# Follow-up steps as own streams, another start, and full-row sample-state products in a hybrid decoder layer

## The chip, the cores and the metric

The kernel runs on one core of a Trainium2 chip. The metric is the device time of one execution, in microseconds. The kernel before took 2090.97 us as the median of three runs (2090.45 to 2092.82).

A core has a matrix engine (TensorE, PE in the profile, with its weight loads as PEld), VectorE (DVE), ScalarE (ACT) and GpSimd (POOL) for elementwise work, and SyncE (SP), which here only issues DMA transfers. Matrix products are collected in PSUM, which has eight banks; everything else lies in SBUF or in device memory.

## The reference

One decoder layer over 1088 tokens: 1024 of a prompt and 64 of a sample group (8 sequences with 8 new tokens, each with 4096 cached tokens in pages).

```
z = x @ w_in                       # 1024 -> 13 parts (q_a k_a v_a q_i k_i w_i q_b k_b v_b g_b a_b gate_a gate_b)
scores = sum_h relu(q_i[h] . k_i) * w_i[h]      # indexer, 8 heads of 64
keys   = the 256 best keys per query            # prompt: causal; sample: the cache and the new tokens
attn   = softmax(q_a . k_a[keys]) @ v_a[keys]   # 8 heads, 2 key heads
log_a  = log_sigmoid(a_b @ w_alpha2 + b) / 16   # per key channel
o_b    = gated linear attention(q_b, k_b, v_b, log_a, state)    # 4 heads, 128 x 256, returns the new state
o_b    = rms_norm(o_b) * g * silu(g_b)
mixed  = (sigmoid(gate_a) * (attn @ w_attn_o) + sigmoid(gate_b) * (o_b @ w_gla_o)) @ w_out
h = layer_norm(alpha * x + mixed);   y = layer_norm(alpha * h + relu(h @ w_ff1)^2 @ w_ff2)
```

It returns y, the new keys, values and indexer keys, and the new states, all in float32.

## The kernel before

**Products.** Each large product is made of three on rounded parts: an operand is split in a high part (h, a rounded copy, ScalarE) and a low part (l, the rest, by a subtraction on VectorE or GpSimd), and h.h, l.h and h.l are added up in one PSUM bank (mm3, L620). Activations lie feature by feature with the tokens along the row, in three chunks of 384, 384 and 320 tokens (CH, L36). One weight tile of 1024 x 128 is thus 8 x 3 products per chunk.

**Jobs.** The projection of x is a list of jobs, one for each weight tile: job 0 (misc: indexer keys, indexer weights and a_b), jobs 1 to 4 (qi, indexer queries), then qa, ka, va, the linear attention's qb, kb, vb, gates of the branch (gb), and the merge gates (gate), with the merge's products (pmb, pma) and the output projection (pwo) behind them. main() (L1701) runs the jobs in order; w_load and w_split read and split weights ahead of their job. fmajor (L629) is one job's chunk.

**Streams.** What depends on results beside the jobs is written as generators: the indexer of the prompt and of the sample (idx_prompt, idx_sample), three searches for the 256th best score (top_first: ga and gb, two groups of prompt queries; top_second; top_sample: gs), the masks made from them, the linear attention (gla, gla_pre), softmax (at_soft) and the value products (at_pv). A search halves an interval: it counts scores over a threshold on VectorE (jk) and ScalarE (jka, jkb) and sets the next threshold in short VectorE steps. The sample search spreads its scores over all partitions and adds the counts up in one small product a step (ppr).

**Order.** No engine chooses its order at run time. A planner (Clock, Stream and Order, L97 to L320) runs the generators against a table of costs and writes one fixed instruction order for each engine. A generator yields the tiles that it needs next. A stream is due when they are ready by the planner's clock, and no earlier than its engines' planned times less a slack:

```
return max([c.ready(x) + self.margin for x in self.need] + [c.t[e] - self.slack for e in self.engines] + [0.0])
```

At each step the first stream of the list that is due goes (L299); a stream with engines=() waits for its tiles alone. PSUM banks go round by last use, and a pinned bank isn't given away. Waits between engines come from tile dependencies. On every queue, SP's too, an instruction that waits holds all behind it.

**Places the change touches.** The start: SP reads the page table, the page rows (ptg), weight 0, x chunk by chunk in pairs of rows, and weight 1 behind chunk 0 (L424 to L480); x is split as it comes; POOL gathers cached indexer pages into cig and SP writes them out (ci_s) to read them again in another layout. The sample state of the linear attention (sample in gla, L1212): pus = k.v for 8 sequences, with 128 rows of k for v's high part and the 64 rows that are not zero for its low part:

```
pe.matmul(pu[:, x * 256:(x + 1) * 256], kz[:, 2 * j + x, :], vh, start=True, stop=False)
pe.matmul(pu[:, x * 256:(x + 1) * 256], kz[:TS, 2 * j + x, :], vl[:TS], start=False, stop=True)
```

The reads of the linear attention's output for the merge (ob_load, L1555: obl, eight blocks, first chunk 0 and then chunks 1 and 2 together, split into obh and obl). The last layer norm of the kernel (ln_last, L1919): sums of y and y squared per token by products with a matrix of ones (plv, pld), the root and its reciprocal, and the product plr which lays the factors along rows.

Nearly every instruction has line L256 in the profile: it is the call in Engine that records it for the planner. So tile names tell places apart.

Of the kernel before, what the change touches and what calls it, by code (L numbers as in the profile page):

```python
# [23 lines left out]
P = 128  # L24
# [3 lines left out]
KT = 8  # L28
# [21 lines left out]
NSH = 6  # L50
# [9 lines left out]
NAHL = 4  # L60
# [20 lines left out]
NGATE = 4  # L81
WLATE = 4.0
# [292 lines left out]
def front(ph, tc, env, A, O):  # L375
# [37 lines left out]

    def scale_rows(x, r):
# [9 lines left out]
    sp.dma_start(ptab, view(A["page_table"], 0, [[0, P], [32, 8], [1, 32]]))  # L424
    ptg = cst("ptg", [P, 2], I32)
    sp.dma_start(ptg, A["page_rows"])
# [3 lines left out]
    def w_load(i):  # L430
        src, kt, m = jobs[i][0]
        pages = []
        for k0 in range(0, kt, 1024 // m):
            kn = min(1024 // m, kt - k0)
            r = page(f"wr{i}_{k0}", F32, [P, kn, m])
            sp.dma_start(r, src[:, k0:k0 + kn, :])
# [3 lines left out]
    def w_split(i):  # L440
        for n, e in enumerate(wt[i]):
# [4 lines left out]
            sub(l, r, f32(h), WLATE if 1 < state["job"] < mix_at - 1 else 0.0)  # L446
            e[0], e[1] = h, l

    state = {"dma": 0, "split": 0, "job": 0}

    def w_get(i):
# [6 lines left out]
        hs, ls = [], []  # L458
        for h, l, kn in wt.pop(i):
            for k in range(kn):  # L460
                hs.append(h[:, k, :])
                ls.append(l[:, k, :])
# [6 lines left out]
    state["dma"] = 1  # L469
# [3 lines left out]
    for c, (c0, n) in enumerate(CH):  # L473
        for k in range(0, KT, 2):
            xr[k, c] = page(f"xr{k}{c}", F32, [P, 2, 384])
            sp.dma_start(xr[k, c][:, :, :n], A["xT"][k:k + 2, :, c0:c0 + n].rearrange("k p t -> p k t"))
        if c == 0:
            w_load(1)
            state["dma"] = 2
# [16 lines left out]
    for g in range(8):  # L496
        dve.tensor_scalar(ix_i[:, g], ptg, 8.0, float(g), op0=OP.mult, op1=OP.add)
    ix_k = const("ix_k", [1, 256], I32)
    dve.tensor_scalar(ix_k, ptab[0:1].rearrange("p a b -> p (a b)"), 128.0, None, op0=OP.mult)
# [32 lines left out]

    for c, (c0, n) in enumerate(CH):
        for k in range(KT):
            s = slice(c0, c0 + n)
# [3 lines left out]
            if c == 0 and k == 0:  # L539
                w_split(0)  # L540
                state["split"] = 1
# [103 lines left out]
    def to_stacks(ps, c, st):  # L645
# [5 lines left out]
        for e in range(2):  # L651
            own, oth = slice(e * 64, e * 64 + 64), slice(64 - e * 64, 128 - e * 64)
            dve.tensor_sub(st[e][oth, c0:c0 + n], ps[own, :n], f32(st[e][own, c0:c0 + n]))
# [4 lines left out]
    def qi_job(f):  # L658
        def run(w):
            st = [page(f"qi{2 * f + e}", F32R) for e in range(2)]  # L660
            for c in range(3):
                ps = yield from fmajor(w, c, f"qi{f}_{c}")
                to_stacks(ps, c, st)
# [4 lines left out]
    def misc_job(w):  # L668
        for c in range(3):
            c0, n = CH[c]  # L670
            ps = yield from fmajor(w, c, f"misc{c}")
# [10 lines left out]
        sp.dma_start(O["kidxT"], misc[0:64])  # L682
        flags.add("misc")
# [11 lines left out]
    def qa_job(f):  # L695
        def run(w):
            st = [page(f"qa{2 * f + e}", F32R) for e in range(2)]
            for c in range(3):
                ps = yield from fmajor(w, c, f"qa{f}_{c}")
                to_stacks(ps, c, st)  # L700
# [55 lines left out]
    def idx_sample():  # L756
# [30 lines left out]
        def chunk(p, kh, kl, n):  # L787
# [7 lines left out]
            dve.scalar_tensor_tensor(rl[:, :n], ps[:, :n], 0.0, f32(rh[:, :n]), op0=OP.max, op1=OP.subtract)  # L795
            return rh, rl

        def sums(p, r, n, po, first, last):
            rh, rl = r
# [4 lines left out]
        for qq in range(4):  # L804
            po = [bank("po0", True), bank("po1", True)]
            pend = None
            for p in range(4):
# [7 lines left out]
                for e in range(2):  # L815
# [3 lines left out]
                    if pend:  # L819
                        yield [pend[1][1]]  # L820
                        sums(*pend)
                    pend = (p, r, 512, po[e], p == 0, p == 3)
            yield [pend[1][1]]
# [8 lines left out]
        for p in range(4):  # L832
            r = chunk(p, kkn[:, 0], kkn[:, 1], 64)
            yield [r[1][:, :64]]
# [140 lines left out]
    def masks(g, qts, gte):  # L975
        for i, grp in enumerate(MKP if not mk else ()):
# [207 lines left out]
    def gla(h):  # L1184
# [17 lines left out]
        dve.tensor_sub(vl[:TS], vs[:TS], f32(vh[:TS]))  # L1202
        qz = small("gqz", 512).rearrange("p (a b) -> p a b", b=TS)
# [8 lines left out]
        def sample():  # L1212
# [4 lines left out]
            for i in range(2):  # L1217
# [8 lines left out]
                for j in range(2):  # L1226
                    yield [kz, vh, vl[:TS]]
                    pu = bank("pus")
                    for x in range(2):
                        pe.matmul(pu[:, x * 256:(x + 1) * 256], kz[:, 2 * j + x, :], vh, start=True, stop=False)  # L1230
                        pe.matmul(pu[:, x * 256:(x + 1) * 256], kz[:TS, 2 * j + x, :], vl[:TS], start=False, stop=True)
                    for x in range(2):
                        b = 2 * j + x
                        la = g["lasts"][:, 4 * i + b:4 * i + b + 1]
                        u = small("us", 256)
                        act.activation(u, pu[:, x * 256:(x + 1) * 256], AF.Copy, scale=la)
                        dve.scalar_tensor_tensor(st[i][:, b, :], st[i][:, b, :], la, u, op0=OP.mult, op1=OP.add)
                sp.dma_start(O["gla_s"][4 * i:4 * i + 4, h].rearrange("b k v -> k b v"), st[i])
# [3 lines left out]
            act.activation(vs[:TS], po[:TS, :256], AF.Copy)  # L1242

# [21 lines left out]
        for ci in range(8):  # L1265
# [20 lines left out]
            else:  # L1286
                S2 = small("S", 256)
                dve.scalar_tensor_tensor(S2, S, g["last"][:, ci:ci + 1], u, op0=OP.mult, op1=OP.add)
                S = S2
            if ci < 7:  # L1290
                Sm = small("Sm", 256)
                act.activation(Sm, S, AF.Copy, scale=g["mid"][:, ci + 1:ci + 2])
# [26 lines left out]

    def g_job(h, j):  # L1320
        def run(w):
# [3 lines left out]
            for c in range(3):  # L1325
                c0, n = CH[c]
                pg = yield from fmajor(w, c, f"gb{h}{j}_{c}")
                t = small("gt")
# [8 lines left out]
                dve.scalar_tensor_tensor(t[:, :n], t[:, :n], 1.0, pg[:, :n], op0=OP.add, op1=OP.mult)  # L1337
                dve.scalar_tensor_tensor(t[:, :n], po[:, :n], gn5[:, j:j + 1], t[:, :n], op0=OP.mult, op1=OP.mult)
                sp.dma_start(ob_s[2 * h + j][:, c0:c0 + n], t[:, :n])
        return run  # L1340

# [40 lines left out]
    def at_soft():  # L1382
# [7 lines left out]
        def norm(x):  # L1390
            rc = tiny("rc", 1)
            dve.reciprocal(rc, x[3][:, 3:4])
            scale_rows(x[2][:, :(x[0][0] + 1) * P], rc)
# [6 lines left out]
        for i, (qt, hp) in enumerate(units):  # L1400
# [11 lines left out]
            for h in range(2):  # L1412
# [18 lines left out]
                if len(fly) > 2:  # L1431
                    yield [fly[0][3][:, 3:4]]
                    norm(fly.popleft())
# [1093 lines left out]
```

## Time and profile before

| | |
|---|---|
| median of three runs | 2090.97 us (2090.45 to 2092.82) |
| the profiled execution | 2094.44 us, span 2092.7 us |
| mean granted TensorE clock | 0.987 |
| TensorE busy | 2039.7 us (97%) in 12443 instructions |
| VectorE busy | 1261.8 us (60%) |
| ScalarE busy | 1121.3 us (54%) |
| GpSimd busy | 774.9 us (37%) |
| DMA | 264.51 MB, mean 126 GB/s |

Times are those of one profiled execution. In a row of the timeline stand the start in us, the length in us, engine, line, operation, out<-in by tile names without their numbers, shape, and in brackets the idle time before it with what ended it; rows with "x8" are eight in a row. A matmul's length overlaps that of the next, so the distance of two starts is what a product costs. A product in float32 that is not rounded shows as two records. The granted clock is 1.00 at full rate and 0.50 at half.

### The profile page before, as it was taken

To read this page: it belongs to the slowest core of one execution; us is meant where nothing else is said; L and a number is where in the kernel's file an instruction comes from. 1 tells how busy PE (TensorE), PEld (TensorE's weight loads), DVE (VectorE), ACT (ScalarE), POOL (GpSimd) and SP (SyncE) were. 2 spreads that over 40 slices of the span, in tenths; PEclk is the share of its full clock that TensorE was granted. 3 is DMA by queue.
4 is the path that set the end of the run, shared out by engine and by line. 5 is a ranking of instruction groups with operands and counts; after the bars stand their busy time and mean duration, and the time that the engine had idled before them with its cause. 6 is when DMAs were issued, how large, how long until landed. Compare 5 with 4: busy or idle time off the path is not lost.

```text
span 2092.7 us, 34594 instructions
## 1 busy us (share of the span) xinstructions
PE 2039.7 (97%) x12443; PEld 1965.4 (94%) x12443; DVE 1261.8 (60%) x2630; ACT 1121.3 (54%) x2222; POOL 774.9 (37%) x579
## 2 busy tenths in 40 slices
PE   7999999999799999999999999999999999999998
PEld 7989999898789999999999899999899999999997
DVE  6976776756845666753167844565654453566635
ACT  5678777787567765674023424455353242445543
POOL 3344121212221113113134324565655343354455
PEclk9999999999899999999999999999999999999998
DMA  6664301212023224245473234655533343235542
GB/s 237 260 188 140 124 21 51 95 34 92 23 72 127 83 83 139 84 135 196 170 277 121 71 89 130 188 155 166 148 100 111 122 130 107 66 129 163 186 151 89
DMA packets 185596, 264.51 MB, mean 126 GB/s; under 512 B 22208, under 2 KB 119488, under 8 KB 185424
## 3 DMA queue, kind: packets, MB, share of 16 engines
q1 hardware_dynamic: 177872, 236.87, 35.1%
q0 software_dynamic: 7552, 25.43, 3.9%
q8 instruction: 98, 1.61, 0.3%
q14 instruction: 74, 0.61, 0.1%
HBM read 212.72 MB, written 49.51 MB: 125 GB/s over the span
## 4 chain that ended last, share of the span: by engine, by line
PE 87%; DVE 5%; issue 4%; POOL 2%; ACT 2%; DMA 1%; SPq 0%; ACTq 0%; POOLq 0%; DVEq 0%
PE pf L256 32%; PE gate L256 9%; PE gb L256 5%; PE pwo L256 4%; PE psv L256 4%; PE pmb L256 4%; PE qb L256 2%; PE kb L256 2%; PE qa L256 2%; PE po L256 2%; PE qi L256 2%; PE psc L256 2%; PE pma L256 2%; PE psq L256 2%; PE pov L256 2%
## 5 line engine op out<-in xcount | busy, mean ns | idle before, releaser
L256 PE MATMUL pf<-a,w 128*128 128x384 f32 (+1 forms) x2304 | 397.4, 328 | 2.3 <-POOL a L256 1.3
L256 PE MATMUL pf<-h,w 128*128 128x384 f32 (+1 forms) x2304 | 396.4, 329 | 3.0 <-POOL w L256 1.7
L256 PEld LDWEIGHTS pf<-h,w 128*128 128x128 f32 x2304 | 380.9, 189 | 5.6 <-POOL w L256 2.1
L256 PEld LDWEIGHTS pf<-a,w 128*128 128x128 f32 x2304 | 378.4, 188 | 6.6 <-POOL a L256 1.8
L256 POOL TENSOR_TENSOR wl<-wr,wh 128x1024 fp32r<-128x1024 f32 (+1 forms) x66 | 150.6, 2283 | 470.0 <-ACT wh L256 415.1
L256 POOL TENSOR_TENSOR w<-wr,w 128x512 fp32r<-128x512 f32 x142 | 202.2, 1433 | 130.6 <-ACT w L256 122.0
L256 ACT ACTIVATE w<-wr 128x512 fp32r<-128x512 f32 x272 | 156.5, 618 | 62.2 <-PE pwo L256 25.8
L256 DVE TENSOR_TENSOR w<-wr,w 128x512 fp32r<-128x512 f32 x130 | 135.0, 1046 | 52.7 <-ACT w L256 52.4
L256 DVE TENSOR_TENSOR acc<-acc,pf 128x384 f32<-128x384 f32 (+1 forms) x136 | 72.9, 538 | 94.9 <-PE pf L256 92.9
L256 PE MATMUL gate<-xh,wh 128*128 128x384 f32 (+1 forms) x384 | 129.9, 338 | 0.0
L256 PE MATMUL gate<-xh,wl 128*128 128x384 f32 (+1 forms) x384 | 125.5, 327 | 0.0
L256 PE MATMUL gate<-xl,wh 128*128 128x384 f32 (+1 forms) x384 | 125.4, 327 | 0.0
L256 POOL TENSOR_TENSOR a<-fr,a 128x384 fp32r<-128x384 f32 (+1 forms) x54 | 52.6, 974 | 195.0 <-ACT a L256 188.5
L256 ACT ACTIVATE wh<-wr 128x1024 fp32r<-128x1024 f32 (+1 forms) x75 | 74.4, 1006 | 76.2 <-DMA wr<-wgo 39.4
L256 DVE TENSOR_TENSOR fr<-fr,pf 128x384 f32<-128x384 f32 (+1 forms) x96 | 50.8, 529 | 91.8 <-ACT fr L256 91.5
L256 ACT ACTIVATE fr<-pf 128x384 f32<-128x384 f32 (+1 forms) x96 | 44.9, 467 | 114.2 <-PE pf L256 112.7
L256 ACT ACTIVATE a<-fr 128x384 fp32r<-128x384 f32 (+1 forms) x96 | 48.7, 507 | 81.1 <-DVE fr L256 79.1
L256 DVE TENSOR_SCALAR_CACHE_REDUCE jk<-sc,ga_f 128x1024 int8<-128x1024 f32 (+2 forms) x96 | 88.4, 921 | 2.1
L256 ACT ACTIVATE jkb<-sc,gb_f 128x896 int8<-128x896 f32 (+2 forms) x96 | 86.0, 896 | 4.4 <-DVE gb_f L256 2.7
L256 DVE TENSOR_TENSOR phl<-ppt,phl 128x512 fp32r<-128x512 f32 (+1 forms) x80 | 50.2, 637 | 60.4 <-ACT phl L256 59.9
L256 PE MATMUL psv<-wh,xh 128*128 128x256 f32 (+1 forms) x288 | 83.8, 291 | 0.0
L256 PE MATMUL psv<-wl,xh 128*128 128x256 f32 (+1 forms) x288 | 81.2, 282 | 0.0
(507 smaller groups left out, 5182.9 us busy)
## 6 DMA issues: line engine op xcount, KB each, us to landing
wr<-wff SPq DMA_DIRECT2D x256, 256.0 KB
wr<-w SPq DMA_DIRECT2D x43, 512.0 KB
ckr<-kT SPq DMA_DIRECT2D x256, 64.0 KB
ga_s<-gate SPq DMA_DIRECT2D x16, 544.0 KB
ci_s<-cig SPq DMA_DIRECT2D x16, 512.0 KB
kir<-ci_s SPq DMA_DIRECT2D x16, 512.0 KB
wr<-wout SPq DMA_DIRECT2D x13, 512.0 KB
mgp<-ga_s SPq DMA_DIRECT2D x16, 384.0 KB
```

The costliest lines, as they stand in the source:

```text
L256: r = f(*a, **k)
```

## The change

**Start.** Weight 0 is read in two halves, each ahead of a pair of x rows; the rest of x's chunk 0 follows, then weight 1 and the page rows, x's chunks 1 and 2, and last the page table. TensorE makes 28 transposes of the identity into a bank that nobody reads (warm). Weight 0 is split half by half between the rows of x, weight 1 after chunk 0, both by ScalarE and VectorE. Jobs 0 and 1 alternate by chunk: misc 0, qi 0, misc 1, qi 1, misc 2, qi 2.

**Follow-ups.** The second halves of steps (the low part of a split weight, of qi and qa, of the indexer's relu, of the softmax weights; the gate's two VectorE steps and its store; the state's update and its store) become streams of their own at the head of the list with no engine limit (task). Where a result is used, force runs what is left of its stream. A bank stays pinned until its low part is read, and some steps wait for a free buffer (room).

**Order of streams.** heads() and decays() (linear attention) stand ahead of the three searches and have no engine limit.

**Sample state.** The low part of v is filled with zeros to 128 rows, and pus takes all of them.

**Others.** One buffer more in one pool and one fewer in another. ob_load starts when all 24 gated outputs are written. In ln_last the sums of blocks 0 to 6 stand apart from the last block's; lsd is added on VectorE; the reciprocal stands ahead of the subtractions.

How the instructions move. On SP at the start (wr are weights, xr pairs of x rows), before:

```order
L256 DMA ptab<-page_table 128x256
L256 DMA ptg<-page_rows 128x2
L256 DMA wr_0_114<-w 128x1024
L256 DMA xr_132<-xT 128x2x384
L256 DMA xr_134<-xT 128x2x384
L256 DMA xr_136<-xT 128x2x384
L256 DMA xr_138<-xT 128x2x384
L256 DMA wr_0_140<-w 128x1024
```

and now:

```order
L257 DMA wr_0_112<-w 128x512
L257 DMA xr_131<-xT 128x2x384
L257 DMA wr_0_112<-w 128x512
L257 DMA xr_134<-xT 128x2x384
L257 DMA xr_136<-xT 128x2x384
L257 DMA xr_138<-xT 128x2x384
L257 DMA wr_0_113<-w 128x1024
L257 DMA ptg<-page_rows 128x2
```

The two tables went behind the weights and x. Further on, the read of job 2's weight stood behind x and ahead of all ci_s writes; now it is here (cig are gathered pages):

```order
L257 DMA ptab<-page_table 128x256
L257 DMA ci_s_171<-cig_292 128x1024
L257 DMA ci_s_171<-cig_294 128x1024
L257 DMA wr_0_384<-w 128x1024
L257 DMA wr_0_386<-w 128x1024
```

It moved behind two writes of gathered pages.

On TensorE, the sample search's product ppr whose predecessor lies on the other side of VectorE's mask work for gb, before:

```order
L256 MATMUL ppr<-gs_p,pm_247 128x2
L256 MATMUL gb_0_5994<-xh_116,wh_0_5580 128x384
L256 MATMUL gb_0_5994<-xl_124,wh_0_5580 128x384
...
L256 MATMUL gb_1_6030<-xh_117,wh_0_5580 128x384
L256 MATMUL gb_1_6030<-xl_125,wh_0_5580 128x384
L256 MATMUL gb_1_6030<-xh_117,wl_0_5581 128x384
L256 MATMUL ppr<-gs_p,pm_247 128x2
```

and now:

```order
L257 MATMUL ppr<-gs_p,pm_283 128x2
L257 MATMUL kb_0_5638<-xh_120,wh_0_5521 128x384
L257 MATMUL kb_0_5638<-xl_128,wh_0_5521 128x384
...
L257 MATMUL gb_0_6032<-xh_115,wh_0_5776 128x384
L257 MATMUL gb_0_6032<-xl_123,wh_0_5776 128x384
L257 MATMUL gb_0_6032<-xh_115,wl_0_5777 128x384
L257 MATMUL ppr<-gs_p,pm_283 128x2
```

31 rows stood between the two ppr; now there are 278: products of kb (54), of the linear attention's values psv (216), of gb (6), and two rows of psa.

On SP where the merge begins (ga_s are stored gates, mgt gates read for the merge, obl the linear attention's outputs), now:

```order
L257 DMA obl_10334<-ob_s_75 128x704
L257 DMA obl_10336<-ob_s_76 128x704
L257 DMA ga_s_93<-gate_10326 128x1088
L257 DMA mgt<-ga_s_86 128x1088
L257 DMA mgt<-ga_s_87 128x1088
L257 DMA obl_10338<-ob_s_77 128x704
L257 DMA obl_10340<-ob_s_78 128x704
L257 DMA obl_10395<-ob_s_79 128x704
L257 DMA obl_10397<-ob_s_80 128x704
L257 DMA obl_10411<-ob_s_81 128x704
L257 DMA obl_10413<-ob_s_82 128x704
```

Before, three second-half reads (128x704) stood ahead of the last gate's write instead of two, and stores of attention outputs stood between the reads that followed. In TensorE's order the last product of the values (pov) stood behind the last gate's products; now it stands ahead of them.

The diff, cut:

```
+    def task(gen):
+        live[:] = [x for x in live if not x.done]
+        live.append(order.add(gen, engines=(), at=len(live)))
+        return gen
+    def room(tag, n):
+        return lambda: not clock.uses or len(clock.free.get(tag, range(99))) >= n
+    def force(gen):
+        for _ in gen:
+            pass
...
-            sub(l, r, f32(h), WLATE if 1 < state["job"] < mix_at - 1 else 0.0)
+            owed.setdefault(i, []).append(task(w_low(l, r, h)))
...
+    for k in range(0, KT, 2):
+        if k < 4:
+            sp.dma_start(w0[:, 2 * k:2 * k + 4], src0[:, 2 * k:2 * k + 4, :])
+        x_in(k, 0)
+    sp.dma_start(wt[1][0][0], jobs[1][0][0])
+    sp.dma_start(ptg, A["page_rows"])
+    for c in (1, 2):
         for k in range(0, KT, 2):
+            x_in(k, c)
+    sp.dma_start(ptab, view(A["page_table"], 0, [[0, P], [32, 8], [1, 32]]))
...
+    warm = bank("warm")
+    for _ in range(WARM):
+        pe.transpose(warm[:, :P], idf, idf)
+    wtop, wnext = halves(0), halves(1)
     for c, (c0, n) in enumerate(CH):
         for k in range(KT):
+            if c == 0 and k in (0, 4):
+                h, l, r = (x[:, k:k + 4] for x in wtop)
+                act.activation(h, r, AF.Copy)
+                dve.tensor_sub(l, r, f32(h))
...
+        clock.pinned.add(ps.tensor.name)
+        def low():
+            for e in range(2):
+                own, oth = slice(e * 64, e * 64 + 64), slice(64 - e * 64, 128 - e * 64)
+                yield [f32(st[e][own, c0:c0 + n])]
+                dve.tensor_sub(st[e][oth, c0:c0 + n], ps[own, :n], f32(st[e][own, c0:c0 + n]))
+            unpin(ps)
+        return task(low())
...
     def misc_job(w):
         for c in range(3):
+            if c:
+                ps = yield from fmajor(q, c - 1, f"qi0_{c - 1}")
+                to_stacks(ps, c - 1, st)
+            if c == 1:
+                w_get(1)
             ps = yield from fmajor(w, c, f"misc{c}")
...
+        pool.memset(f32(vl[TS:]), 0.0)
...
-                        pe.matmul(pu[...], kz[:TS, 2 * j + x, :], vl[:TS], start=False, stop=True)
+                        pe.matmul(pu[...], kz[:, 2 * j + x, :], vl, start=False, stop=True)
...
+                task(gated_out(h, j, c, t, pg, po))
...
+                pend.append((kt, m, hl, task(low(hl, pt, m))))
...
-        yield lambda: state["job"] >= merge_at - OBLEAD
+        yield lambda: state["job"] >= merge_at - OBLEAD and outs[0] == 24
...
+    s_gl = order.add(heads(), engines=(), margin=M_GL)
+    order.add(decays(), engines=(), margin=M_GL)
     s_tq = order.add(top_second(), engines=("act",), slack=1.0)
     s_tp = order.add(top_first(), engines=("dve",), slack=1.0)
     s_la = order.add(later(), engines=("dve",), slack=0.5)
-    s_gl = order.add(heads(), margin=M_GL)
-    order.add(decays(), margin=M_GL)
...
             if f == 6:
-                pool.tensor_tensor(sd, sd, z[6], op=OP.add)
+                dve.tensor_tensor(sd, sd, z[6], op=OP.add)
...
+                cols(pw, 3, sd)
+                yield [s2]
+                cols(pw, 0, s2)
...
+        yield [r3[:, :3]]
+        dve.reciprocal(r3[:, :3], r3[:, :3])
         ds = small("lds")[:, :n]
         act.activation(ds, pd[:, :n], AF.Copy)
-        dve.tensor_tensor(z[0], z[0], pd[:, :n], op=OP.subtract)
-        dve.reciprocal(r3[:, :3], r3[:, :3])
...
-        for f in range(1, 5):
+        for f in range(5):
```

More of the change, by code (lines that the diff above doesn't have):

```diff
@@ L445, in w_split, with w_low @@
             act.activation(h, r, AF.Copy)
-            sub(l, r, f32(h), WLATE if 1 < state["job"] < mix_at - 1 else 0.0)
+            owed.setdefault(i, []).append(task(w_low(l, r, h)))
             e[0], e[1] = h, l
+    owed = {}
+    def w_low(l, r, h):
+        yield [f32(h)]
+        sub(l, r, f32(h), WLATE if 1 < state["job"] < mix_at - 1 else 0.0)
     state = {"dma": 0, "split": 0, "job": 0}
@@ L458, in w_get @@
         hs, ls = [], []
+        for x in owed.pop(i, ()):
+            force(x)
         for h, l, kn in wt.pop(i):
@@ L468, in front @@
     w_load(0)
-    state["dma"] = 1
+    w_load(1)
+    state["dma"] = 2
     xh = [env["xpage"](f"xh{k}", F32R, (P, T)) for k in range(KT)]
@@ L538, in front @@
             dve.tensor_sub(xl[k][:, s], r, f32(xh[k][:, s]))
-            if c == 0 and k == 0:
-                w_split(0)
-                state["split"] = 1
+        if c == 0:
+            h, l, r = wnext
+            act.activation(h, r, AF.Copy)
+            dve.tensor_sub(l, r, f32(h))
+            for g in range(8):
+                dve.tensor_scalar(ix_i[:, g], ptg, 8.0, float(g), op0=OP.mult, op1=OP.add)
+    dve.tensor_scalar(ix_k, ptab[0:1].rearrange("p a b -> p (a b)"), 128.0, None, op0=OP.mult)
+    state["split"] = 2
     def iota_f(name, shape, pattern, base=0):
@@ L794, in chunk, with low @@
             act.activation(rh[:, :n], ps[:, :n], AF.Relu)
[L795 to L796 removed]
+            clock.pinned.add(ps.tensor.name)
+            def low():
+                yield [f32(rh[:, :n])]
+                dve.scalar_tensor_tensor(rl[:, :n], ps[:, :n], 0.0, f32(rh[:, :n]), op0=OP.max, op1=OP.subtract)
+                unpin(ps)
+            return rh, rl, task(low())
         def sums(p, r, n, po, first, last):
[L799 removed]
+            rh, rl = r[:2]
             w = wsel[:, p].rearrange("p e b -> p (e b)")
@@ L975, in masks @@
     def masks(g, qts, gte):
+        if not mk:
+            yield room("pg", 4)
         for i, grp in enumerate(MKP if not mk else ()):
@@ L1242, in sample, with update @@
             act.activation(vs[:TS], po[:TS, :256], AF.Copy)
+        def update(us, out, t):
+            for u, x, la in us:
+                yield [u]
+                dve.scalar_tensor_tensor(x, x, la, u, op0=OP.mult, op1=OP.add)
+            if out is not None:
+                sp.dma_start(out, t)
         def quads(i):
@@ L1460, in tail, with low @@
                              f32(hl[e * 64:e * 64 + 64].rearrange("p (h q) -> p h q", q=P)))
+        def low(hl, pt, m):
+            yield [f32(hl[:, 0, :256 * m])]
+            dve.tensor_sub(hl[:, 1, :256 * m], pt, f32(hl[:, 0, :256 * m]))
+            unpin(pt)
         def step():
@@ L1936, in ln_last, with cols @@
         s2, sd = small("ls2")[:, :n], small("lsd")[:, :n]
-        pv, pd = bank("plv", True), bank("pld", True)
+        pv, pw, pd = bank("plv", True), bank("plw", True), bank("pld", True)
+        def cols(p, i, x):
+            for j, o in enumerate(off):
+                pe.matmul(p[:, i + j:i + j + 1], x[:, o:o + P], on[:, :1], start=True, stop=True)
         for f in range(8):
```

124 lines of the change are left out of this document (79 added, 45 removed).

## Prediction

> **What bounds the kernel now.** I read the page first, then TensorE's waits, then busy time by stretches of 50 us, and last the timelines of the stretches that are not full.
>
> ```profile
> PE 2039.7 (97%) x12443; PEld 1965.4 (94%) x12443; DVE 1261.8 (60%) x2630; ACT 1121.3 (54%) x2222; POOL 774.9 (37%) x579
> ```
>
> TensorE is busy 97% of the span and the next engine 60%. So the work on TensorE sets the time, and a change can win in three ways only: less TensorE work, less idle time on it, or less time at a low clock. The waits say who ended its idle time (total us, times, longest):
>
> ```profile
> PE ppr L256 <- ACT jka L256: 11.5, 2, 8.6
> PE misc L256 <- ACT wh L256: 8.4, 1, 8.4
> PE pov L256 <- ACT phl L256: 4.6, 2, 2.7
> ```
>
> The stretches where they lie (after the times: length, busy time of PE, PEld, DVE, ACT, POOL, then the granted clock):
>
> ```profile
> core 0: us, PE busy (x) PEld busy (x) DVE busy (x) ACT busy (x) POOL busy (x), PEclk, DMA share, GB/s
> 0.00:50.00 50.00, 38.60 (x192) 36.87 (x193) 31.57 (x76) 27.04 (x56) 17.21 (x24) 0.93 0.68 235
> 550.00:600.00 50.00, 38.51 (x207) 34.96 (x205) 35.46 (x59) 28.92 (x60) 21.09 (x14) 0.86 0.15 47
> 900.00:950.00 50.00, 45.04 (x285) 43.36 (x284) 27.84 (x94) 37.26 (x95) 10.10 (x10) 0.92 0.57 183
> ```
>
> Idle time is 11.4, 11.5 and 5.0 us there, in all 27.9 of the span's 2092.7, and a low clock stands beside it. These three stretches, the end of the kernel, and one group of slow products (pus) are what the change touches with a price.
>
> **Term 1, the start.**
>
> ```profile
> 1.74 0.44 SPq L256 DMA_DIRECT2D wr<-w  x1
> 4.00:8.00 4.00, 0.00 (x0) 0.00 (x0) 1.39 (x10) 1.11 (x2) 0.00 (x0) 1.00 1.00 372
> 6.89 0.52 ACT L256 ACTIVATE xh<-xr 128x384 fp32r<-128x384 f32 x1 [4.79 <-DMA xr<-xT]
> 8.41 0.69 PE L256 MATMUL misc<-xh,wh 128*128 128x384 f32 x1 [8.41 <-ACT wh L256]
> 8.45 2.35 POOL L256 TENSOR_TENSOR wl<-wr,wh 128x1024 fp32r<-128x1024 f32 x1 [6.97 <-ACT wh L256]
> 11.34 0.52 PE L256 MATMUL misc<-xh,wh 128*128 128x384 f32 x1
> 11.66 0.52 PE L256 MATMUL misc<-xl,wh 128*128 128x384 f32 x1
> 8.81 10.72 DVE L256 TENSOR_TENSOR xl<-xr,xh 128x384 fp32r<-128x384 f32 x19 [0.80 <-ACT xh L256]
> 29.30 0.34 PE L256 MATMUL qi<-xh,wl 128*128 128x384 f32 x1
> 29.47 0.33 PE L256 MATMUL qi<-xh,wh 128*128 128x384 f32 x1
> 43.24 0.31 PE L256 MATMUL qi<-xh,wl 128*128 128x320 f32 x1
> 43.39 0.34 PE L256 MATMUL qi<-xh,wh 128*128 128x384 f32 x1
> ```
>
> The first product starts at 8.41 us, the third waits for POOL's 2.35 us, and the stream then runs 0.32 us apart (11.34, 11.66), where the full rate is 0.17 (29.30, 29.47) for 384 columns and 0.15 (43.24, 43.39) for 320. The product of 43.39 is the first of job 2. Jobs 0 and 1 are 144 products, 96 of 384 columns and 48 of 320: 96 x 0.173 + 48 x 0.147 = 23.7 us, so 43.4 us holds 19.7 us of something else.
>
> In the changed order the first half weight and the first x pair are 0.65 MB ahead of the first product, not 0.90 MB, and they stand two small loads earlier on SP's queue. At 372 GB/s that is 0.7 us of transfer. The first weight's issue, at 1.74 behind two loads that begin SP's queue at 0.8, moves 0.9 us forward. So x is there at about 5.2, not 6.9. Then VectorE sets the pace of chunk 0: eight xl at 0.56 (10.72/19) and two halves of wl, which I scale from it by columns (512/384 x 0.56 = 0.75): 6.0 us, from 5.8 to about 11.8. The second weight's wl, 1.5 by the same scale, ends at 13.3, with its products already running, so job 1's chunk 0 ends near 16.7. Then x is ahead and TensorE is the bound: 48 products of 384 (8.3) and 48 of 320 (7.1) end at 32.1, with 1 us for the small pw and pww products at 33.1. Before: 43.4. Gain 10.3.
>
> Against it: the load for job 2 now stands on SP behind two writes of gathered pages, which must wait for POOL's gathers, and the gathers' indices are computed after chunk 0. If the load lands at 30 rather than 26, job 2 waits up to 4 us with 2 us at half rate behind it. I take -9, bounds -4 and -10.3. What hides the later gathers is the 10 us of work that is now ahead of their use; if that is short, it is this same loss.
>
> The 28 warming transposes lie before x arrives, on an idle engine: cost nothing. If they leave the clock as it is, chunk 0's 24 products run 0.32 apart from about 6.9 until some 5.5 us later (17 of them), and the rest at full rate: end at 13.6 instead of 11.8 to 13.3, some 1.5 us later. By the Trainium skill, "TensorE: Matmul & The Clock Gate", Part 4 (PE-mode transpose), a transpose doesn't count as activity for the clock gate, which would make this part of the change idle. No run here shows it yet; by it the start term would be -7.5.
>
> **Term 2, pus.** The sample-state products alternate a 128-row and a 64-row operand.
>
> ```profile
> L256 PE MATMUL pus<-gvl,gkz x32: 379/380/382, 307.1 to 625.7; 64*128 64x256 f32 x32
> ...
> 307.10 0.38 PE L256 MATMUL pus<-gvl,gkz 64*128 64x256 f32 x1
> 307.41 0.38 PE L256 MATMUL pus<-gvh,gkz 128*128 128x256 f32 x1
> 307.72 0.38 PE L256 MATMUL pus<-gvl,gkz 64*128 64x256 f32 x1
> 308.03 0.44 PE L256 MATMUL kb<-xh,wh 128*128 128x384 f32 x1
> 548.69 0.28 PE L256 MATMUL psv<-wh,xh 128*128 128x256 f32 x1
> 548.81 0.28 PE L256 MATMUL psv<-wl,xh 128*128 128x256 f32 x1
> ```
>
> They stand 0.31 us apart, where psv, of the same columns and type with 128 rows throughout, stands 0.12. With all rows at 128 nothing alternates. Of 64 products (32 of each kind, in 16 groups of four) I count three of each four at 0.19 saved, since the first follows another type of product anyway: 48 x 0.19 = 9.1, and half for the rest, 1.5: -10.6. Bounds: 0 (the 0.31 is of these operands, whatever the rows) and -12.2 (all 64). I take -10. The four extra memsets are on POOL, 37% busy.
>
> **Term 3, the search at 550 us.**
>
> ```profile
> 545.59 0.15 DVE L256 TENSOR_TENSOR gb_m<-gb_n,gb_l 128x3 int32<-128x3 f32 x1
> 567.61 0.22 DVE L256 TENSOR_SCALAR gs_m<-ppr 128x1 int32<-128x1 f32 x1
> ...
> 562.14 0.34 PE L256 MATMUL gb<-xh,wl 128*128 128x384 f32 x1
> 571.04 0.59 PE L256 MATMUL ppr<-gs_p,pm 128*128 128x2 f32 x2 [8.56 <-ACT jka L256]
> 571.49 0.67 PE L256 MATMUL gb<-xh,wh 128*128 128x384 f32 x1
> 576.44 0.38 PE L256 MATMUL gb<-xh,wh 128*128 128x384 f32 x1
> ```
>
> The sample search (gs) makes one small product ppr per step. Its next step needs VectorE's gs_m, which stands behind 22.0 us of mask work (545.59 to 567.61), and TensorE has only 31 rows, about 5.5 us, between the two ppr. It idles, and 16 products from 571.49 to 576.44 are 0.32 apart (2.4 us lost); the earlier wait cost 10 such products (1.5). Sum: 11.5 idle + 3.9 = 15.4. VectorE's burst is in the new order unchanged, but 278 rows of TensorE lie between the ppr on its two sides: 39 products of 384 columns (6.7), 25 of 320 (3.7) and 216 of 256 (25.5 at 0.118), 35.9 us. The burst of 22.0, the four cu steps now behind it and the count on ScalarE fit in that. I take -15, bounds 0 (the stall comes back at another ppr) and -15.4.
>
> **Term 4, from gates to merge.** In 900 to 950, 5.0 us idle and at most 4 us of low clock (0.08 x 50) go to pov, which has no gate products left beside it. In the new order the last pov stands ahead of the last gate, so these some 8 us go. But the merge now begins right at the last gate, and on SP the last gate's write, two reads of gates (0.56 MB each) and six second-half loads of 0.36 MB each stand in a row behind that gate's result: 3.8 MB.
>
> ```profile
> 4.15 0.66 DVE L256 TENSOR_SCALAR ix_i<-ptg 128x2 int32<-128x2 int32 x8 [2.05 <-DMA ptg<-page_rows]
> 940.00:945.00 5.00, 1.77 (x6) 1.17 (x6) 2.01 (x8) 3.68 (x12) 0.72 (x1) 0.67 0.96 298
> ```
>
> At 298 GB/s that is 12.8 us, so with 2 us to start (VectorE's wait of 2.05 for a small load) the last lands 14.8 after the gate; without a wait the product is due 4.2 us (chunk 0) + 7 x 0.52 = 7.8 after it. A wait of up to 7, less if the queue runs ahead. Before, the idle time itself gave these loads their lead. Net -2, bounds -8 and +3.
>
> **Term 5, the end.**
>
> ```profile
> 2077.24 0.49 DVE L256 TENSOR_TENSOR acc<-acc,pf 128x320 f32<-128x320 f32 x1 [1.74 <-PE pf L256]
> 2079.07 0.36 PE L256 MATMUL plv<-on,lsd 128*128 128x1 f32 x2
> 2079.29 0.36 PE L256 MATMUL plv<-on,acc 128*128 128x1 f32 x2
> 2083.23 0.17 DVE L256 RECIPROCAL lr<-lr 128x3 f32<-128x3 f32 x1
> ```
>
> Each of the 12 plv groups takes 0.22. Six of them now go ahead of the last block (1.3 us), lsd no longer waits for POOL, and a subtraction of 0.5 is no longer in front of the reciprocal. It comes about 2.5 sooner, and the five subtractions then behind it give back 0.5: -2, bounds 0 and -2.6.
>
> **Costed at nothing**: the low halves as own streams. They move VectorE work of the same length; VectorE is 60% busy, its cover is TensorE's queue of full products, and the price without cover is the slower rival's below.
>
> **Sum**: -9 - 10 - 15 - 2 - 2 = -38. The profiled run took 2094.4 us, 3.5 over the median of 2091.0, with a span of 2092.7; the difference is carried over to the median: 2053.
>
> **Rivals.** (a) *The transposes don't lift the clock*: start -7.5, 2054.5. For it: the low rate at the start is seen only with an engine that was idle. (b) *The pus interval is the operands' own*: -28, 2063. For it: no row has these operands with 128 rows; against: psv's 0.12. (c) *Two loads are the new waits*: job 2's weight (start -4) and the merge (+3): -28, 2063. For it: SP's order; against: TensorE's queue may run later than I count. (d) *The search stall returns elsewhere*, the change of order not doing what it says here: -23, 2068. (e) *Slower*: a bank of PSUM is now held until the low half has its turn on VectorE; about 160 steps hold one (80 phl, 32 rl, 24 halves of qi and qa, 24 gates), and TensorE waits for a bank where VectorE is in a burst like that of 22 us. From 38/160 = 0.24 us per step it eats the gain; at 0.3 it is +10, 2101. For it: bursts; against: TensorE waits for no bank in the list above. (f) Gains and losses cancel: 2091.
>
> **Numbers.** Forecast 0.39, (a) 0.18, (b) 0.10, (c) 0.13, (d) 0.08, (e) 0.07, (f) 0.05. What this kernel's measurement can tell is about 0.2%, 4 us. Faster holds the first five, 0.88; same 0.05; slower 0.07. Low end: all best bounds, -10.3 - 12.2 - 15.4 - 8 - 2.6 = -48.5, 2042. High end: (b) and (c) together, -18, 2073, and one new stall of the search's kind (7): 2080. Outside lie (e), (f) and little else.
>
> **What would show it.** Right: the first product of job 2 near 34, pus 0.12 apart, no wait for jka over 1 us, the reciprocal within 3.5 us of the last acc. Wrong: waits of job 2's products for wh or wl, pmb waiting for obh or obl over 5 us, a wait for phl or rl in many short pieces, or a low clock in stretches that were full before.

## The result and the profile after

| kernel | median | span of the profiled execution |
|---|---|---|
| before | 2091.64 us (2090.45 to 2092.82, 4 runs) | 2092.7 us |
| changed | 2074.57 us (2073.64 to 2076.12, 4 runs) | 2073.4 us |

The ratio is 0.9919, 95% interval 0.9902 to 0.9936: 17 us faster. The direction was forecast, the size was not: 38 us were. The time lies at the upper part of the range of 2042 to 2080.

TensorE's line of the page and its waits, after:

```profile
PE 2029.4 (98%) x12471; PEld 1962.7 (95%) x12471; DVE 1268.5 (61%) x2638; ACT 1111.2 (54%) x2215; POOL 784.1 (38%) x585
```

```profile
PE pw L257 <- ACT misc L257: 7.0, 2, 4.2
PE pwo L257 <- DVE mg L257: 4.0, 3, 2.9
PE psas L257 <- DVE gb_m L257: 3.5, 1, 3.5
PE pmb L257 <- ACT obh L257: 2.9, 1, 2.9
```

The search's 11.5 us for jka and the 8.4 at the very start are gone. In their place stand 7.0 us of pw (1.4 before), 3.5 us of psas and 2.9 us of pmb (both not in the list before). The stretches, after, in the same columns as before:

```profile
0.00:50.00 50.00, 40.65 (x210) 38.48 (x211) 29.48 (x73) 26.20 (x54) 24.99 (x28) 0.86 0.90 319
300.00:350.00 50.00, 46.57 (x339) 44.71 (x337) 38.45 (x98) 37.69 (x83) 11.15 (x6) 1.00 0.19 56
350.00:400.00 50.00, 48.41 (x269) 43.63 (x270) 37.23 (x109) 40.66 (x98) 8.10 (x6) 0.93 0.16 52
550.00:600.00 50.00, 50.00 (x295) 45.33 (x294) 20.68 (x45) 35.88 (x81) 15.16 (x10) 1.00 0.20 65
900.00:950.00 50.00, 46.80 (x262) 45.26 (x261) 16.22 (x29) 19.70 (x39) 15.49 (x9) 0.93 0.65 237
```

550 to 600 is full at full clock. The first 50 us hold 2 us more TensorE work than before (38.60); the transposes alone are busy for 4.9. The clock there reads 0.86, not 0.93, but the column does not cover the first microseconds: before, it reads 1.00 from 8 to 16 us, where products stand 0.32 apart. So the two first stretches can't be compared by it. And 300 to 400, which was full, has 5.0 us idle and a low clock.

Where the time went is read from the first and last start of groups that stand alike in both orders (va is job 6, pmb the merge, pf the first MLP product; a row has length and then first and last start). Before:

```profile
L256 PE MATMUL va<-xh,wh x24: 303/334/525, 127.2 to 144.7; 128*128 128x384 f32 x16, 128*128 128x320 f32 x8
...
L256 PE MATMUL pmb<-obh,wh x192: 306/334/668, 946.8 to 1044.8; 128*128 128x384 f32 x128, 128*128 128x320 f32 x64
...
L256 PE MATMUL pf<-h,w x2304: 303/334/687, 1152.7 to 2048.2; 128*128 128x384 f32 x128, 128*128 128x320 f32 x64
```

After:

```profile
L257 PE MATMUL va<-xh,wh x24: 306/334/346, 127.6 to 141.3; 128*128 128x384 f32 x16, 128*128 128x320 f32 x8
...
L257 PE MATMUL pmb<-obh,wh x192: 306/334/686, 922.3 to 1023.8; 128*128 128x384 f32 x128, 128*128 128x320 f32 x64
...
L257 PE MATMUL pf<-h,w x2304: 303/334/630, 1132.7 to 2030.4; 128*128 128x384 f32 x128, 128*128 128x320 f32 x64
```

| up to | before | after | moved | forecast |
|---|---|---|---|---|
| va, first (the start is over) | 127.2 | 127.6 | +0.4 | -9 |
| pmb, first (pus, the search and pov too) | 946.8 | 922.3 | -24.5 | -42 (-9 -10 -15 -8) |
| pmb, last (the merge's reads too) | 1044.8 | 1023.8 | -21.0 | -36 |
| pf, first | 1152.7 | 1132.7 | -20.0 | -36 |
| end | 2092.7 | 2073.4 | -19.3 | -38 |

So half of the gap is the start, which won nothing, and most of the other half arose between va and pmb. A single trace places va to some 3 us only: with the old start it comes at 127.2, 123.9 (e4) and 125.9 (e11), with the new start as it stands in the changed kernel at 127.0 to 129.3 (this trace, e3, e6, e7, e9, e10). So the new start came out some 2 us later on average, not sooner.

**The start.** SP, POOL, ScalarE and TensorE after:

```profile
14.60 6.54 POOL L257 DMA_INDIRECT cig<-ciT,ix_i  x1 [0.30 <-DVE xl L257]
25.07 0.33 SPq L257 DMA_DIRECT2D ci_s<-cig  x1
25.49 1.32 SPq L257 DMA_DIRECT2D wr<-w  x2
35.07 1.06 ACT L257 ACTIVATE wh<-wr 128x1024 fp32r<-128x1024 f32 x1 [11.38 <-DMA wr<-w]
40.02 0.38 PE L257 MATMUL pw<-idf,misc 8*128 8x8 f32 x2 [2.84 <-ACT misc L257]
40.33 0.69 PE L257 MATMUL qi<-xh,wh 128*128 128x384 f32 x1
44.00:48.00 4.00, 4.00 (x13) 3.44 (x13) 2.98 (x9) 2.29 (x5) 1.74 (x4) 0.50 0.97 305
```

POOL's second gather stood 6.54 us in its queue while VectorE made xl. The write of its page was issued at 25.07, and only behind that SP issued job 2's weight, which landed at 35.0. ScalarE waited 11.4 us for it with misc's evacuations queued behind, pw waited for these, and job 2 began at 40.33 (43.39 before). Then 9 us ran at half rate (the last row: a clock of 0.50, 13 instructions in 4 us).

### The profile page after: what moved, and what is told of

It reads as the page before. It is cut to its first block, busy times and chain, and to the rows that moved or that the text cites. A ratio compares the mean times of both kernels' runs of the same rounds, so it can differ in the third digit from the quotient of the medians.

```text
span 2073.4 us, 34621 instructions
## 1 busy us (share of the span) xinstructions
PE 2029.4 (98%) x12471; PEld 1962.7 (95%) x12471; DVE 1268.5 (61%) x2638; ACT 1111.2 (54%) x2215; POOL 784.1 (38%) x585
## 4 chain that ended last, share of the span: by engine, by line
PE 52%; issue 3%; DVE 2%; POOL 1%; ACT 1%; DMA 0%; SPq 0%; ACTq 0%; POOLq 0%; DVEq 0%
PE pf L257 34%; PE pmb L257 4%; PE pwo L257 4%; PE gate L257 2%; PE psc L257 2%; PE pma L257 2%; PE pob L257 1%; PE pst L257 1%; POOL w L257 0%; DVE w L257 0%; DVE aqz L257 0%; POOL wl L257 0%; PE pov L257 0%; SPq L257 0%; DMA obl<-ob_s 0%
## 5 line engine op out<-in xcount | busy, mean ns | idle before, releaser
L257 PE MATMUL psv<-wh,xl 128*128 128x256 f32 (+1 forms) x288 | 81.2, 282 | 0.0
```

The source lines that it names most:

```text
L257: r = f(*a, **k)
```

## The experiments

Three sets (e1 to e4, e5 to e8, e9 to e12), each on one chip with its own runs of the kernel before, whose medians were 2090.61, 2097.33 and 2094.65 us; ratios are to these, and times of different sets compare by ratios. The changed kernel has 0.9919 on the chip of the result and 0.9900 in e9. Where a span or a start is compared, it is that of the profiled execution.

| run | median | ratio, 95% interval |
|---|---|---|
| e1 job 2's weight early | 2073.15 | 0.9919 (0.9902 to 0.9935) |
| e2 e1 without transposes | 2074.80 | 0.9930 (0.9914 to 0.9947) |
| e3 streams put back | 2087.12 | 0.9986 (0.9976 to 0.9995) |
| e4 before, full-row pus alone | 2091.14 | 1.0005 (0.9995 to 1.0014) |
| e5 e1 and small vectors early | 2063.73 | 0.9848 (0.9818 to 0.9877) |
| e6 psas later | 2077.13 | 0.9910 (0.9883 to 0.9937) |
| e7 obl early | 2067.60 | 0.9863 (0.9835 to 0.9890) |
| e8 before, new start alone | 2106.41 | 1.0048 (1.0028 to 1.0068) |
| e9 the changed kernel again | 2074.68 | 0.9900 (0.9882 to 0.9918) |
| e10 changed, pus on 64 rows | 2084.79 | 0.9958 (0.9941 to 0.9974) |
| e11 before, stream order alone | 2125.55 | 1.0152 (1.0131 to 1.0173) |
| e12 e5 and e7 | 2056.16 | 0.9817 (0.9801 to 0.9834) |

**e1, job 2's weight read early**

```
     for f in range(1, 4):
         job(wtile(f), qi_job(f), lambda f=f: len(qis) <= QIS)
+    w_load(2)
+    state["dma"] = 3
```

> The changed kernel with one thing moved: the read of job 2's weight is issued on SP right behind the page table, ahead of the writes of gathered pages. Theory: the start lost its gain because that read stood behind those writes (ScalarE waited 11.4 us for it, TensorE 7.0 us in pw, then half rate). Then the first product of job 2 comes near 33.5 us (40.3 in the changed kernel), pw waits under 1 us, and the time falls by 7 to 10 us, to about 2066. Rival: the indexer's chain of gathers, writes and reads, or DMA bandwidth, sets the end of this part anyway; then the gain comes back as a wait for kir near 125 us, and the time stays within 2 us of 2074.6.

Job 2 began at 33.59, as the prediction had it, and pw did not wait. Yet va began at 129.1, no sooner than in the changed kernel, and the ratio is the same, 0.9919. The gain came back as two other waits, up to 100 us:

```profile
PE psi L257 <- DVE qi L257: 4.9, 1, 4.9
PE psi L257 <- ACT r L257: 3.6, 2, 3.3
```

The rival held, though the wait was not kir's. What VectorE waited for, and where that load stood on SP:

```profile
46.29 18.99 SPq L257 DMA_DIRECT2D ci_s<-cig  x8
66.59 0.49 SPq L257 DMA_DIRECT2D gn<-gla_norm_g  x1
70.57 0.17 DVE L257 TENSOR_SCALAR gn<-gn 128x2 f32<-128x2 f32 x1 [10.18 <-DMA gn<-gla_norm_g]
```

A load of 128 x 2 numbers stood behind eight writes of gathered pages, and 10.2 us of VectorE's queue behind it. The same queue, another victim: e5 takes that up.

**e2, e1 without the transposes** (WARM = 0)

> As e1 (job 2's weight read early), and without the 28 transposes ahead of the first product. Theory: the transposes lift the clock, so without them the first products stand 0.32 us apart for some 5 us and the time is 1 to 3 us above e1. Rival: transposes don't count as activity; then the spacing of the first products and the time are those of e1 within 0.5 us.

The first products stand 0.32 us apart without them, and 0.17 with them. Without:

```profile
12.24 0.52 PE L257 MATMUL misc<-xl,wh 128*128 128x384 f32 x1
12.56 0.52 PE L257 MATMUL misc<-xh,wl 128*128 128x384 f32 x1
```

With them, in the changed kernel, two stretches (17 transposes in 3.55 us, then 11 instructions, two of them begun earlier, in 1.00; the clock column reads 1.00 in both, so the rate is read from the counts):

```profile
1.45:5.00 3.55, 3.55 (x17) 3.55 (x18) 1.29 (x7) 1.28 (x2) 1.08 (x6) 1.00 0.86 272
5.20:6.20 1.00, 1.00 (x11) 1.00 (x10) 0.61 (x2) 0.77 (x2) 0.00 (x0) 1.00 0.94 299
```

and its first products:

```profile
6.56 0.34 PE L257 MATMUL misc<-xl,wh 128*128 128x384 f32 x1
6.73 0.34 PE L257 MATMUL misc<-xh,wl 128*128 128x384 f32 x1
```

So the transposes lifted the rate (0.21 us each up to about 5.1 us, 0.11 behind), and the theory holds on the mechanism. In time e2 is 1.7 us above e1, but the two intervals overlap, and va begins at 128.7 in e2 and at 129.1 in e1: what the transposes win in the first 15 us can't be seen 110 us later, and their worth isn't shown.

**e3, linear attention's streams back behind the searches**

```
-    s_gl = order.add(heads(), engines=(), margin=M_GL)
-    order.add(decays(), engines=(), margin=M_GL)
...
     s_la = order.add(later(), engines=("dve",), slack=0.5)
+    s_gl = order.add(heads(), margin=M_GL)
+    order.add(decays(), margin=M_GL)
```

> The changed kernel with the linear attention's two streams put back behind the searches, with their old engine limits. Theory: this order alone took the search's stall away and brought the new wait of psas; then a wait of ppr for jka of several us returns, the wait of psas (3.5 us and 3 at half rate) goes, and the time rises by 5 to 10 us, to 2080 to 2085. Rival: the stall went because of the follow-up streams; then it stays away, psas no longer waits, and the time falls by 5 to 7, to about 2068.

12.5 us slower than the changed kernel by the medians, 14 us slower than e1 on the same chip. The theory had 5 to 10, the rival a fall. A stall behind VectorE's queue is back, but at another instruction, and psas waits more, not less:

```profile
449.60 0.45 PE L257 MATMUL psas<-gq,gk 128*64 128x64 f32 x2 [5.28 <-DVE gk L257]
485.87 0.69 PE L257 MATMUL gb<-xh,wh 128*128 128x384 f32 x1 [11.28 <-DVE gt L257]
```

gt is the gated output of the linear attention; it stands behind at least 15 us of VectorE's mask work for gb, as ppr did before. So the stream order is needed for the search's gain, and the wait of psas isn't its doing alone: with the new order and no follow-ups (e11) psas waits 3.3 us, with follow-ups and the old order 5.3, and in the kernel before it isn't in the list.

**e4, the kernel before with full-row pus alone**

```
+        pool.memset(f32(vl[TS:]), 0.0)
...
-                        pe.matmul(pu[...], kz[:TS, 2 * j + x, :], vl[:TS], start=False, stop=True)
+                        pe.matmul(pu[...], kz[:, 2 * j + x, :], vl, start=False, stop=True)
```

> The kernel before with one part of the change alone: the sample-state products take all 128 rows for the low part, filled with zeros. Theory: the alternation of 128 and 64 rows is what costs 0.31 us a product; the products stand 0.12 apart and the time falls by 9 to 12 us, to about 2081. Rival: the products get faster, but waits of the planned order around them take it back; then less than 5 us.

The products got cheaper and the time didn't change: 1.0005. The last gate product comes at 923.8, 12.6 us sooner than before, but the last pov at 944.7, only 7.8 sooner, and the first pf at 1146.3, 6.4 sooner; the rest of the kernel, untouched, took 942.7 us instead of 940.0. Of what was gained, 3.3 us were there at va already (123.9), ahead of anything that was changed, so pus itself won some 9 us up to the gates, 4.5 up to pov and 3 up to pf. TensorE reached the searches and the attention earlier, and they were not ready:

```profile
PE ppr L256 <- ACT jka L256: 16.1, 4, 7.0
...
PE pov L256 <- ACT phl L256: 5.9, 4, 2.9
```

These were 11.5 and 4.6. The rival held. The profiled run of before lay 3.8 us above the median of its 19 runs here, so what the trace shows of the last 4 us isn't told apart from scatter; the 2.7 us behind pf go with a low clock (0.86 over 25 us) behind a wait of psc, which that run of before didn't have (last section).

**e5, small vectors read early too**

```
     w_load(2)
     state["dma"] = 3
+    sp.dma_start(b_al, A["b_alpha"])
+    sp.dma_start(gn5, A["gla_norm_g"])
+    sp.dma_start(env["lnp"], A["ln"])
```

(and the three lines taken out of later().)

> As e1 (job 2's weight read early), and the three small loads of bias, norm and scale vectors, too, are issued ahead of the writes of gathered pages. In e1 the start's gain was there at 45 us and gone at 80: VectorE waited 10.2 us for one of these loads, which stood behind eight of those writes, and TensorE 4.9 us for VectorE. Theory: SP's queue alone takes the start's gain; then the lost time up to 150 us falls by 6 to 7 against e1 and the time to 2065 to 2068. Rival: the next link of the gather chain takes it again; then within 2 us of e1's 2073.

```profile
L257 PE MATMUL va<-xh,wh x24: 306/334/346, 119.9 to 133.7; 128*128 128x384 f32 x16, 128*128 128x320 f32 x8
...
L257 PE MATMUL pf<-h,w x2304: 303/334/630, 1124.6 to 2019.8; 128*128 128x384 f32 x128, 128*128 128x320 f32 x64
```

va begins 7.7 us sooner than in the changed kernel and pf 8.1; the span is 10.7 us shorter, the rest being psc's wait, after which the clock stayed full here (last section). Of SP's loads, four moved, and the start has most of the gain that was forecast for it: va comes 7.3 us sooner than in the traced kernel before, where 9 were forecast. The theory holds: it was SP's queue. One wait of 2.0 us of psi remains there.

**e6, psas later**

```
         yield [q, k]
+        if h == 1:
+            yield lambda: clock.t["pe"] >= max(clock.ready(q), clock.ready(k)) + 6.0
         ps = bank("psas")
```

> The changed kernel with the second linear attention head's first products (psas) written some 38 rows of TensorE later (about 6 us of products). Theory: psas waited 3.5 us and cost 3 at half rate because VectorE's gk, in a queue with the searches and held by POOL's gq, came later than the planned order has it; with 6 us more the wait goes and the time falls by 4 to 7 us, to about 2069. Rival: the searches around it then stall in its place; within 2 us of the changed kernel.

psas no longer waits, but the searches do, 4.5 us in two waits, the longer one near 548 us:

```profile
PE ppr L257 <- ACT jka L257: 4.5, 2, 2.8
```

The ratio is 0.991, as without the edit, though its interval, some 5 us either way, leaves room for a few. The trace points the same way: from va to pmb it takes 796.9 us here and 794.7 in the changed kernel. The rival held: in this stretch VectorE and ScalarE set the pace for long enough that a wait taken away at one place stands at another.

**e7, the linear attention's output read early**

```
-OBLEAD = 1
-OBFLY = 3
+OBLEAD = 2
+OBFLY = 8
```

> The changed kernel with the reads of the linear attention's output (obl) issued one job earlier and up to eight in flight; TensorE's order is the same. Theory: pmb's wait (2.9 us, and about 3 at half rate) is for reads that stand behind the last gate's write; it goes, and the time falls by 4 to 6 us, to about 2070. Rival: the reads then hold up the gates' stores or softmax data, or the next wait of the merge (pwo for mg) grows by as much; within 2 us.

SP with the last reads and the last gate's write:

```profile
912.91 1.67 SPq L257 DMA_DIRECT2D obl<-ob_s  x2
922.91 0.32 SPq L257 DMA_DIRECT2D ga_s<-gate  x1
```

and the merge's products:

```profile
L257 PE MATMUL pmb<-obh,wh x192: 306/334/338, 922.2 to 1016.6; 128*128 128x384 f32 x128, 128*128 128x320 f32 x64
```

All reads are now issued 8 us ahead of the last gate's write. pmb begins as in the changed kernel (922.2) and takes 94.4 us instead of 101.5: the wait for these reads and the half rate behind it cost 7.1 us. pf comes 5.4 us sooner; the rest stands in pwo's waits for mg, so each side was right in part. The span is 7.8 us shorter, 2.4 of it behind pf, where the clock stayed full after psc's wait here too.

**e8, the kernel before with the new start alone** (half loads, transposes, alternating chunks)

> The kernel before with the new start alone: half loads, transposes, alternating chunks, and the page table behind x. Follow-up steps and stream order are the old ones. Theory: the start alone wins nothing, since job 2's weight then waits behind the gathered pages: lost time up to 150 us within 2 us of before, and a time within 4 us of before. Rival: the loss came from the follow-up streams' evacuations; then the start alone gains 6 to 9 us.

Slower by 0.5%. va begins at 122.9, 4.3 sooner than in the traced kernel before and 1.0 sooner than in e4, which has the old start. But the merge begins at 955.7, 8.9 later than before. The last gate product still comes 5 us sooner (931.6); the last pov, behind it, comes 8 us later (960.2), so the loss arose at the attention's end. ppr waits 8.5 us, 3.0 less than before; more than before wait:

```profile
PE pov L257 <- ACT phl L257: 6.2, 4, 2.6
PE pw L257 <- ACT misc L257: 5.6, 2, 3.0
```

The theory holds for pw's wait. Its bounds fail: va moved by 1 to 4 us, not within 2, and the time lies 9 us over before, not within 4. The rival's gain of 6 to 9 us isn't there either. va stands 4 to 6 us sooner than with the same start in the changed kernel, so the rest of the change costs some of the start; what in it was not tried.

**e9 and e10, the changed kernel again, and with the old pus.** e10's edit is that of e4 turned round; TensorE's order is otherwise the same.

> The changed kernel as it is, beside the next three on one chip, since the kernel before read 2090.6 on one chip and 2097.3 on another. All theories: 0.992 of the kernel before.

> The changed kernel with the sample-state products back on 64 rows for the low part; TensorE's order is otherwise the same. Theory: the products alone cost 10 to 12 us here as in the kernel before, and here no wait behind them takes it back, so the time rises by 9 to 12 us over e9. Rival: what the products save comes back as waits of the linear attention and the searches, as in e4; then less than 4 us.

10.1 us between them; the intervals are apart. In the changed kernel the products' saving arrives whole. The same edit won nothing in the kernel before.

**e11, the kernel before with the new stream order alone**

> The kernel before with the linear attention's streams ahead of the searches and without engine limits, nothing else. Theory: this order takes away the search's stall near 550 us by itself: ppr waits under 3 us for jka, and the time falls by 10 to 16 us. Rival: it needs the follow-up streams too; then another stall of the same sort stands elsewhere, and the time is within 5 us of before.

31 us slower. The search's stall is gone: ppr waits 0.3 us. But now pov waits twelve times, and twelve more for the low halves (4.1 us), and gb once for a weight:

```profile
PE pov L256 <- ACT phl L256: 11.8, 12, 1.7
...
PE gb L256 <- POOL wl L256: 7.8, 1, 7.8
```

Neither theory: the order does remove the stall, and without the follow-up streams it costs more at the attention's end than it wins.

**e12, e5 and e7 together**

> The changed kernel with the early reads of e5 (job 2's weight and three small vectors) and of e7 (the linear attention's output). Theory: the start's 8 us and the merge's 7 are in different places and add up: 14 to 18 us under e9. Rival: the second is eaten by pwo's wait for mg; then 10 to 12.

2056.16 us, 18.5 us under e9 on the same chip; they add up, a little over the 14 to 18 of the theory. It is the fastest kernel here, 0.9817 of before. That this is 3 us from the forecast says nothing for the forecast: two edits that the change doesn't have made it.

## Why the prediction was wrong

**The sum** failed in its first term, and in what it left out.

**Term 1, -9, came out as +0.4.** The rates, the DMA and VectorE's pace were right: chunk 0's last product came at 11.61, job 1's chunk 0 ended at 16.7 (as forecast), and all of jobs 0 and 1 by 32. What failed is the step "if the load for job 2 lands at 30 rather than 26, job 2 waits up to 4 us": it landed at 35.0, and pw waited 7.0 with 9 us of half rate behind it. The step was loose by the figures at hand as well: job 2 was wanted at 33.1, and a weight that lands at 30 is split by 31.1 (1.06 on ScalarE) and 33.4 (2.35 on POOL), so that landing would have cost next to nothing. I had taken the two gathers for done in time. POOL's second one took 6.54 us, and then the weight's transfer shared the DMA with four more gathers, which runs at 386 to 414 GB/s in all between 28 and 40 us. And the bound stopped at one load: e1 freed that load, and the next one behind the same writes (gn) took the gain; only e5, with all four moved, got 7.7 against the changed kernel. Rival (c) had this mechanism with the wrong size.

**Rival (a)** fell: the transposes lift the rate, and e2 shows the first products without them at 0.32. How much time that saves isn't shown. The Trainium skill, "TensorE: Matmul & The Clock Gate", Part 4 (PE-mode transpose), says that transposes don't count as activity for the clock gate. Here 28 transposes of a 128 x 128 float32 tile did; the measurement decides.

**Term 2, -10**, is 10.1 in the changed kernel (e10 against e9). The products in the new trace stand 0.12 apart:

```profile
304.24 0.28 PE L257 MATMUL pus<-gvl,gkz 128*128 128x256 f32 x1
304.36 0.28 PE L257 MATMUL pus<-gvh,gkz 128*128 128x256 f32 x1
```

The count of three in four and a half gave 10.6. (Rival (b) says that no row had these operands with 128 rows; the rows with gvh had, and stood 0.31 from their neighbours. What no row had is 128 rows in both.) What the term didn't say is that it holds only where nothing waits behind: alone it is worth nothing (e4).

**Term 3, -15**, came out: ppr doesn't wait for jka any more, and 550 to 600 us is full. By e3 and e11 it needs the stream order, and the order needs the follow-up streams.

**Term 4, -2**: the parts were right (pov's wait went, the merge's first products wait for the six reads behind the gate's write), at 7.1 us for the reads where I had up to 7. The merge itself took 3.5 us more than before.

**Term 5, -2**: from the last acc to the first scaling step 6.35 us instead of 7.90, so -1.6. That step before, and then the end after:

```profile
2085.14 3.76 DVE L256 SCALAR_TENSOR_TENSOR acc<-acc,lnp,plr 128x320 f32<-128x320 f32 x8 [0.17 <-PE plr L256]
...
2059.49 0.49 DVE L257 TENSOR_TENSOR acc<-acc,pf 128x320 f32<-128x320 f32 x1 [0.65 <-PE pf L257]
2063.52 0.17 DVE L257 RECIPROCAL lr<-lr 128x3 f32<-128x3 f32 x1 [0.36 <-ACT lr L257]
2065.84 3.75 DVE L257 SCALAR_TENSOR_TENSOR acc<-acc,lnp,plr 128x320 f32<-128x320 f32 x8
```

The reciprocal comes 4.0 us after the last acc (6.0 before), not within 3.5.

**Left out: psas.** "Costed at nothing" covered the moved streams as a whole, and no stretch was priced for the second linear attention head. Its first product waits for gk on VectorE, which stands behind search steps there (psas starts at 350.78; the step gb_m, which the wait is put down to, ran just behind gk):

```profile
348.68 1.96 DVE L257 TENSOR_TENSOR gk<-gk,cu 128x1088 f32<-128x1088 f32 x1 [0.36 <-POOL gvl L257]
```

3.5 us idle, and a clock of 0.93 over the 50 us behind it: some 7 us together. e6 shows that it can't be taken away by itself. From va to pmb the pieces are -15.4 for the search, -10.1 for pus, -8 for pov's gap and +7 for psas, -26.5 in all, where the landmarks have -24.9; the 1.6 left lies in short waits of pov and gb that were not told apart.

**Carried over**: the 3.5 us between the profiled run of before and its median belonged to that run. In the changed kernel the same difference is 0.5, so taking 3.5 off the forecast made 3 us of the miss. From pf to the end both kernels take about the same, 940.0 and 940.7 us, although the end is 1.6 shorter. The same wait of 2.5 us in psc was followed by a low clock in one and not in the other (below).

## What to carry to other kernels

When TensorE is freed early in a kernel, ask of every queue what waits at its head: a transfer that depends on a gather holds all loads behind it on SP, small ones too, and the gain moves from one of them to the next until all are ahead of it. Price a saving in products by what stands behind it: the same 10 us were worth nothing where searches and softmax were late anyway, and all of it where they weren't. A reorder of a plan has to be read as a whole, with its other parts in place: the start alone and the stream order alone each made the kernel slower, and taking the stream order out of the whole (e3) did too.

## What the runs showed of the hardware that was not expected

Transposes on TensorE raise its rate: 28 of them, from 1.45 us on, ran 0.21 us apart up to about 5.1 us and 0.11 apart behind, and the products behind them at full rate at once. Without them (e2) the products stood 0.32 apart up to 14.8 us.

A wait of 2 to 2.5 us is enough for the low clock, but doesn't always bring it. Before, pss waits 2.01 us, and the first products of va behind it stand 0.32 apart until 129.4:

```profile
125.36 0.50 PE L256 MATMUL pss<-kir,qz 128*128 128x512 f32 x1 [2.01 <-DVE kir L256]
127.16 0.53 PE L256 MATMUL va<-xh,wh 128*128 128x384 f32 x1
127.48 0.53 PE L256 MATMUL va<-xl,wh 128*128 128x384 f32 x1
```

In e4 the same wait is 1.28 us, and va runs at full rate. psc waits 2.5 us for aqz in every trace here. Behind it the clock is full in before, e5, e7, e8, e9 and e11, and low in the other eight (0.86 or 0.93 over the 25 us in which it lies). The changed kernel had both, low in its first trace and full in e9:

```profile
1425.00:1475.00 50.00, 46.95 (x260) 43.66 (x259) 27.97 (x56) 22.26 (x42) 26.00 (x22) 0.93 0.44 123
1425.00:1475.00 50.00, 46.86 (x278) 44.49 (x277) 31.48 (x61) 23.05 (x44) 28.31 (x24) 1.00 0.46 133
```

Some 0.07 x 50 = 3.5 us hang on that in a single execution, which a comparison of two traces has to allow for. How much of the scatter between runs it makes isn't shown: e9's span is 2.1 us longer than the first trace's, with the full clock there. Why it falls one way or the other was not tried.

A gather on POOL took 6.54 us where its neighbours took 0.94 to 1.22, while VectorE ran subtractions without a pause (16 of xl in 7.05 us, from 13.26 on). The ten other traces with the new start have it again (5.66 to 6.54). But such subtractions alone don't hold a gather: before, two gathers took 1.23 us (from 12.16) and 1.31 (from 13.69) in the middle of VectorE's unbroken run of 8.81 to 19.5. What held this one was not tried.
